# One level of Strassen's algorithm in the second product of four feed-forward layers

## The chip, the cores and the metric

The kernel runs on one core of one Trainium2 chip. What is compared is the time of one execution on the device, in microseconds (us). TensorE (PE) multiplies matrices into PSUM banks, VectorE (DVE) and ScalarE (ACT) work on tiles in SBUF and PSUM, GpSimd (POOL) does a little, and SyncE (SP) issues most of the loads from memory.

## The reference

Two blocks of a network run one after the other on a sequence of 512 tokens of width 1024, in float32. The second block has two layers, and each layer has two feed-forward parts around a mixer. Those four feed-forward parts are the place of the change:

```python
D_FF = 2816
def swiglu_half(x, w1, w3, w2):
    return 0.5 * ((jax.nn.silu(x @ w1) * (x @ w3)) @ w2)

for l in range(2):
    x = layer_norm(ALPHA * x + swiglu_half(x, ffn1_w1[l], ffn1_w3[l], ffn1_w2[l]), ln1_g[l], ln1_b[l])
    ...                                       # mixer, and its own layer norm
    x = layer_norm(ALPHA * x + swiglu_half(x, ffn2_w1[l], ffn2_w3[l], ffn2_w2[l]), ln3_g[l], ln3_b[l])
```

Here x is 512 x 1024, w1 and w3 are 1024 x 2816, and w2 is 2816 x 1024. "The hidden values" are silu(x w1) * (x w3); "the second product" is hidden values times w2.

## The kernel before, in words

Every large product is done in three passes of a rounded type. An operand is split into a high part and a low part (`split`, lines 212 to 215: ACT copies the value to the type `F32R`, DVE subtracts that copy from the value), and `mm3` (lines 240 to 243) adds three matmuls for one: low x high, high x low, high x high. So each 128 x 128 by 128 x 512 step is three matmuls, and each weight tile costs one ACT and one DVE operation before PE can use it.

A feed-forward layer (`ffn`, line 804) goes over the 2816 hidden columns in 11 blocks of 256: block 0 alone, then the pairs (1, 2), (3, 4), (5, 6), (7, 8) and (9, 10). `hidden(c)` makes one block's hidden values: two pieces of w1 and w3 (1024 x 256 each, loaded in halves of 512 KB) against the transposed x, 96 matmuls in four PSUM banks of the pool "mm" (three banks), then on ACT the silu, on DVE the product, and the split into `hh` and `hl`. These lie with the hidden column on the partitions, so that 128 tokens of them are the stationary operand of the second product. For a pair, both hidden blocks come first. Then the second product goes over 4 token tiles x 2 halves of the 1024 output columns; each of the 8 results adds 4 steps of 128 hidden columns (12 matmuls) into a bank of the pool "mx" (five banks), and DVE adds the bank to the residual `xr` (line 848). After the last pair, `lnorm` does the layer norm.

The order in which instructions stand in each engine's queue is set when the kernel is built: a scheduler takes the program, a model of each operation's cost and the free buffers, and puts what it holds to be ready first. Each queue is then worked off strictly in order, and waits on semaphores keep data and buffers safe. Tiles come from pools: a tile of a tag with `bufs=n` waits until one of that tag's n places is released. The pool `WP` has 2 staging tiles (`wst`) and 4 places each for high (`wh`) and low (`wl`) weights; the layer's own weight pool has 3 and 5. All weight loads are issued by SP, in order.

Of the kernel before, what the change touches and what calls it, by code (L numbers as in the profile page):

```python
# [133 lines left out]
def build(ctx, tc, A, out, stage="all"):  # L134
# [24 lines left out]
    def nm(s):  # L159
        uid[0] += 1  # L160
        return f"{s}{uid[0]}"
# [18 lines left out]
    def mmbank():  # L180
        return bank("mm")

    def mxbank():
        return bank("mx")
# [108 lines left out]
    def nat(t):  # L293
        return slice(t * 128, (t + 1) * 128)
# [437 lines left out]
        return nxt  # L732


    def lnorm(t, po, scale, g, b, pl, done):
# [9 lines left out]
        xn = pl.tile([128, D], F32, tag="lnx", name=nm("lnx"), bufs=1)  # L745
        sq = pl.tile([128, D], BF16, tag="lnq", name=nm("lnq"), bufs=1)
# [9 lines left out]
        hc = slice(h * 512, (h + 1) * 512)  # L756
        nc.sync.dma_start(out[0, nat(t), hc], A["xr"][:, t, hc])

    def ln_rows(pl, names, l):
        o = []  # L760
        for n in names:
            r = pl.tile([128, D], F32, name=nm("lnr"))
            nc.scalar.dma_start(r, rows(A[n][l]))
            o.append(r)
        return o
# [6 lines left out]
    def open_ffn(l, f, pre=None):  # L772

        es, w = pre[0:2] if pre else (ExitStack(), None)
        w = w or weights(es, 3, 5, "right")
        return es, w, [Piece(A[f"{f}_{n}_2"][l], 0, 8, 0, 256, wp) for n, wp in (("w1", w), ("w3", WP if pre else w))], []
# [15 lines left out]
    def hidden_half(pl, pre, n0, bufs, sa=None):  # L792

        if not pre[3]:
            pre[3].extend(hidden_tiles(pl, bufs))
# [5 lines left out]
        sa = (pl.tile([128, T], F32, tag="sa", name=nm("sa"), bufs=2) if sa is None else sa).rearrange("p (j n) -> p j n", j=2)  # L801
        act(sa, ab[0], ab[1], hh[:, :, n0:n0 + 256], hl[:, :, n0:n0 + 256])

    def ffn(l, f, ln, pre, ahead=None, scale=None):
# [5 lines left out]
        esf = ExitStack()  # L810
        banks(esf, mm=3, mx=5)
        fp = pool(esf, nm("ffn"), "right", LINE)
        g, b = ln_rows(fp, (ln + "_g_2", ln + "_b_2"), l)

        def hidden(c):

            if c == 0:
                for n0 in (256,) if pre[3] else (0, 256):
                    hidden_half(fp, pre, n0, 3)
                return pre[3]  # L820
            pcs = [Piece(w, 0, 8, c * 256, 256, wf) for w in (w1, w3)]
            hh, hl = hidden_tiles(fp, 3)
            for j in range(2):
                ab = [mmbank() for _ in range(2)]
                for i in range(2):
                    prod(ab[i], pcs[i], j, 0, T)
                act(fp.tile([128, T], F32, tag="sa", name=nm("sa"), bufs=2), ab[0], ab[1], hh[:, j, :], hl[:, j, :])
            return hh, hl

        for cs in ((0,), (1, 2), (3, 4), (5, 6), (7, 8), (9, 10)):  # L830
            hs = [hidden(c) for c in cs]
            p2 = [Piece(w2, 2 * c, 2, 0, 1024, wf if c == 10 else WP) for c in cs]
            if 10 in cs and ahead:
                nxt = ahead(pre)
            nk = 2 * len(cs)
            for t in range(NT):
# [12 lines left out]
                if 10 in cs:  # L849
                    if t > 0 and ahead:  # L850
                        next_tile(t - 1, scale)
                    lnorm(t, lambda h: pos[h], 0.5, g, b, fp, None if ahead else put_out)
        if ahead:
            next_tile(3, scale)
        esf.close()
# [7 lines left out]
    def mixer(l, pre, ahead=None, scale=None):  # L863
# [655 lines left out]
                next_tile(t - 1, scale)  # L1519
            lnorm(t, lambda h: po[h], 1.0, g, b, P4, None if ahead else put_out)  # L1520
        if ahead:
            hidden_half(pool(nxt[0], nm("hid"), "right", LINE), nxt, 0, 1,
                        P4.tile([128, D], F32, tag="lnx", name=nm("sa"), bufs=1)[:, 0:T])
            B["mx"] = B["gd"]
            next_tile(2, scale)
            next_tile(3, scale)
# [51 lines left out]
```

## Time and profile before

| | |
|---|---|
| median of 3 runs | 2773.11 us (2770.71 to 2774.16) |
| the profiled execution | 2771.1 us, span 2769.3 us |
| PE busy | 2722.5 us, 98% of the span, 14736 matmuls |
| DVE busy | 1399.8 us, 51% |
| ACT busy | 999.7 us, 36% |
| POOL busy | 185.8 us, 7% |
| mean DMA rate | 94 GB/s, 16 engines' mean share 31% |

The span runs from the first to the last instruction; the execution's time has a little around it. Busy shares are means over stages with different limits, so a stage is to be read by itself. A PE that is shown busy need not run at its peak, because matmuls overlap: its rate is read from the distance between starts.

### The profile page before, as it was taken

To read this page: it belongs to the slowest core of one execution; us is meant where nothing else is said; L and a number is where in the kernel's file an instruction comes from. 1 tells how busy PE (TensorE), PEld (TensorE's weight loads), DVE (VectorE), ACT (ScalarE), POOL (GpSimd) and SP (SyncE) were. 2 spreads that over 40 slices of the span, in tenths; PEclk is the share of its full clock that TensorE was granted. 3 is DMA by queue.
4 is the path that set the end of the run, shared out by engine and by line. 5 is a ranking of instruction groups with operands and counts; after the bars stand their busy time and mean duration, and the time that the engine had idled before them with its cause. 6 is when DMAs were issued, how large, how long until landed. Compare 5 with 4: busy or idle time off the path is not lost. (4 is left out here: it accounts for less than half of the span.)

```text
span 2769.3 us, 36863 instructions
## 1 busy us (share of the span) xinstructions
PE 2722.5 (98%) x14736; PEld 2224.0 (80%) x14736; DVE 1399.8 (51%) x2698; ACT 999.7 (36%) x1607; POOL 185.8 (7%) x319
## 2 busy tenths in 40 slices
PE   8999999999999999999999999999999999999998
PEld 6779887888888887777888888888887777788887
DVE  6655555344433346865633435334354866643334
ACT  4444553333222234553422224222234553422222
POOL 1000013000000001110100000000000201100000
PEclk9999999999999999999999999999999999999999
DMA  5122222343333223224423333333323323433331
GB/s 165 47 77 70 69 77 88 104 156 101 104 102 91 76 87 91 64 72 138 128 92 95 102 101 99 91 92 97 102 66 89 94 59 129 132 97 92 92 91 46
DMA packets 195003, 260.64 MB, mean 94 GB/s; under 512 B 14376, under 2 KB 153264, under 8 KB 194768
## 3 DMA queue, kind: packets, MB, share of 16 engines
q1 hardware_dynamic: 169200, 221.55, 27.0%
q10 hardware_dynamic: 25632, 36.74, 4.1%
q8 instruction: 116, 1.90, 0.3%
q14 instruction: 55, 0.45, 0.0%
HBM read 246.09 MB, written 11.11 MB: 93 GB/s over the span
## 5 line engine op out<-in xcount | busy, mean ns | idle before, releaser
L215 DVE TENSOR_TENSOR wl<-wst,wh 128x1024 fp32r<-128x1024 f32 (+2 forms) x434 | 516.3, 1192 | 521.4 <-ACT wh L214 520.7
L167 PE MATMUL mm<-xTh,wl 128*128 128x512 f32 (+1 forms) x1984 | 749.6, 378 | 2.2 <-ACT xTh L214 2.1
L167 PE MATMUL mm<-xTl,wh 128*128 128x512 f32 (+1 forms) x1984 | 749.5, 378 | 0.6 <-DVE xTl L215 0.6
L167 PE MATMUL mm<-xTh,wh 128*128 128x512 f32 (+1 forms) x1984 | 746.4, 376 | 0.0
L214 ACT ACTIVATE wh<-wst 128x1024 fp32r<-128x1024 f32 (+2 forms) x434 | 438.9, 1019 | 778.4 <-PE mx L167 327.1
L167 PEld LDWEIGHTS mm<-xTh,wl 128*128 128x128 f32 x1984 | 373.7, 189 | 70.7 <-ACT xTh L214 2.6
L167 PEld LDWEIGHTS mm<-xTl,wh 128*128 128x128 f32 x1984 | 373.8, 188 | 70.3 <-issue 2.9
L167 PEld LDWEIGHTS mm<-xTh,wh 128*128 128x128 f32 x1984 | 373.8, 188 | 66.5
L167 PE MATMUL mx<-wh,hl 128*128 128x512 f32 x704 | 276.6, 393 | 0.0
L167 PE MATMUL mx<-wl,hh 128*128 128x512 f32 x704 | 274.1, 389 | 0.0
L167 PE MATMUL mx<-wh,hh 128*128 128x512 f32 x704 | 271.5, 390 | 0.0
L167 PE MATMUL mm<-wh,xTl 128*128 128x512 f32 (+2 forms) x640 | 254.0, 398 | 0.4 <-DVE xTl L215 0.4
L167 PE MATMUL mm<-wl,xTh 128*128 128x512 f32 (+2 forms) x640 | 248.8, 389 | 0.0
L167 PE MATMUL mm<-wh,xTh 128*128 128x512 f32 (+2 forms) x640 | 245.7, 384 | 0.0
L848 DVE TENSOR_TENSOR xr<-xr,mx 128x512 f32<-128x512 f32 x160 | 109.5, 686 | 206.8 <-PE mx L167 206.8
L789 DVE TENSOR_TENSOR sa<-sa,mm 128x512 f32<-128x512 f32 x88 | 60.5, 687 | 276.7 <-PE mm L167 276.7
L167 PEld LDWEIGHTS mm<-wl,xTh 128*128 128x128 f32 x640 | 144.7, 226 | 18.2 <-issue 5.8
L167 PEld LDWEIGHTS mm<-wh,xTl 128*128 128x128 f32 x640 | 144.2, 226 | 18.7 <-issue 5.2
L167 PEld LDWEIGHTS mx<-wh,hl 128*128 128x128 f32 x704 | 132.1, 188 | 32.3 <-DVE hl L215 5.7
L167 PEld LDWEIGHTS mm<-wh,xTh 128*128 128x128 f32 x640 | 144.7, 226 | 14.5 <-issue 1.8
L167 PEld LDWEIGHTS mx<-wh,hh 128*128 128x128 f32 x704 | 132.1, 188 | 27.8
L167 PEld LDWEIGHTS mx<-wl,hh 128*128 128x128 f32 x704 | 132.2, 188 | 26.5
(396 smaller groups left out, 2731.7 us busy)
## 6 DMA issues: line engine op xcount, KB each, us to landing
wst<-in_ffn_w_dram SPq DMA_DIRECT2D x264, 512.0 KB, 3.7
wst<-in_w_in_dram SPq DMA_DIRECT2D x106, 512.0 KB, 3.7
wst<-in_w_out_dram SPq DMA_DIRECT2D x24, 512.0 KB, 3.4
xd<-xr ACTq DMA_DIRECT2D x8, 512.0 KB, 2.6
wst<-in_w_in_dram SPq DMA_DIRECT2D x16, 256.0 KB, 2.8
lnr<-in_ln_g_dram ACTq DMA_DIRECT2D x6, 512.0 KB, 4.2
lnr<-in_ln_b_dram ACTq DMA_DIRECT2D x6, 512.0 KB, 6.0
ya<-xd ACTq DMA_DIRECT2D x10, 256.0 KB, 2.9
```

Source lines behind the costliest of these rows:

```text
L167: PE.matmul(o, a, b, start=start, stop=stop)
L214: S.activation(hi, src, AF.Copy)
L215: V.tensor_sub(lo, src, hi.bitcast(F32))
L789: V.tensor_mul(sa, sa, pb)
L848: V.tensor_add(xs, xs, po)
```

## The change

In each of the four feed-forward layers the second product of the pairs (1, 2), (3, 4), (5, 6) and (7, 8) is done by one level of Strassen's algorithm, in Winograd's form. The hidden values of a pair are a 2 x 2 array (tokens 0 to 255 and 256 to 511, first and second block); the matching 512 rows of w2 are a 2 x 2 array of quarters (256 rows by 512 columns). Seven products of quarters take the place of eight. Hidden values go in as x1 (tokens 0 to 255 of the first block, "11", and the difference s3), x2 ("12" and "22"), x3 (s2 and s1) and x4 (s4); weights as the quarters 11, 21 and 22 and the sums t1 to t4. Each sum is made in float32 before it is split.

Three of the seven products ("12" by 21, s4 by 22, "22" by t4) belong to one quarter of the output each, and DVE adds them to `xr` straight from PSUM. The other four belong to more than one. They are kept in SBUF tiles (`acc`, 256 tokens x 512 columns each) over all four pairs of the layer, and `joined` adds them to `xr` once, after the last of these pairs. In the first pair ACT copies these four into their tiles; later DVE adds to them.

The layer norm's gain and offset rows are now loaded after that, into the places of `acc`, and its scratch tiles take places of hidden tiles. Blocks 0, 9 and 10 are done as before. The core of the diff (left out: the passing of tags, and of one pool that lets every third set of hidden tiles lie with block 0's):

```diff
+        def raw(c):
+            pcs = [Piece(w, 0, 8, c * 256, 256, wf) for w in (w1, w3)]
+            sa = fp.tile([128, 2, T], F32, tag="sa", name=nm("sa"), bufs=2)
+            for j in range(2):
+                ab = [mmbank() for _ in range(2)]
+                for i in range(2):
+                    prod(ab[i], pcs[i], j, 0, T)
+                S.activation(sa[:, j, :], ab[0], AF.Silu)
+                V.tensor_mul(sa[:, j, :], sa[:, j, :], ab[1])
+                yield sa, j
...
+        def quarters(c):
...
+            for i, j in ((0, 0), (1, 1), (0, 1), (1, 0)):
+                q = (wp if i == j else fp).tile([128, 2, 512], F32, tag="wst", name=nm("wst"), bufs=2)
+                r = (2 * c + 2 * i) * 128
+                nc.sync.dma_start(q, w2[r:r + 256, j * 512:(j + 1) * 512].rearrange("(k p) c -> p k c", p=128))
...
+            parts("11", q11)
+            V.tensor_add(q11, q11, q12)
+            V.tensor_add(q12, q12, q22)
+            parts("t3", q12)
+            parts("21", q21)
+            parts("22", q22)
+            V.tensor_add(q22, q22, q11)
+            V.tensor_add(q21, q21, q22)
+            parts("t1", q11)
+            parts("t2", q22)
+            parts("t4", q21)
...
+        def pair(c):
...
+            V.tensor_sub(s3, sa1[:, :, lo], sa1[:, :, up])
+            split(x1h[:, :, lo], x1l[:, :, lo], sa1[:, :, lo])
+            split(x1h[:, :, up], x1l[:, :, up], s3)
+            w = quarters(c)
+            for sa2, _ in raw(c + 1):
+                pass
+            V.tensor_sub(sa1[:, :, up], sa1[:, :, up], sa2[:, :, up])
+            x2h, x2l = tiles()
+            split(x2h, x2l, sa2)
+            V.tensor_sub(sa1[:, :, lo], sa1[:, :, up], sa1[:, :, lo])
+            V.tensor_add(sa2[:, :, lo], sa2[:, :, lo], sa1[:, :, lo])
...
+            split(x4h, x4l, sa2[:, :, lo])
+            x3h, x3l = tiles()
+            split(x3h, x3l, sa1)
...
+            for x, y, to in (("11", "11", "q1"), ("s3", "t3", "q7"), ("12", "21", (0, 0)), ("s4", "22", (0, 1)),
+                             ("s1", "t1", "q5"), ("s2", "t2", "q6"), ("22", "t4", (2, 0))):
...
+                for t in range(2):
+                    po = mxbank()
+                    for k in range(2):
+                        mm3(po, xh[:, k, nat(t0 + t)], xl[:, k, nat(t0 + t)], wh[:, k, :], wl[:, k, :], k == 0, k == 1)
+                    if type(to) is not str:
+                        o = xr[:, to[0] + t, to[1] * 512:(to[1] + 1) * 512]
+                        V.tensor_add(o, o, po)
+                    elif new:
+                        S.activation(acc[to][:, t, :], po, AF.Copy)
+                    else:
+                        V.tensor_add(acc[to][:, t, :], acc[to][:, t, :], po)
+
+        def joined():
...
+            V.tensor_add(u2, u2, q1)
+            to(0, 0, q1, ALU.add)
+            to(0, 1, q5, ALU.add)
+            to(0, 1, u2, ALU.subtract)
+            V.tensor_add(u2, u2, q7)
+            to(2, 0, u2, ALU.add)
+            to(2, 1, q5, ALU.add)
+            to(2, 1, u2, ALU.subtract)
 
         for cs in ((0,), (1, 2), (3, 4), (5, 6), (7, 8), (9, 10)):
+            if 0 < cs[0] < 9:
+                pair(cs[0])
+                continue
+            if 10 in cs:
+                joined()
             hs = [hidden(c) for c in cs]
```

What this does to the queues, in the pair of blocks 3 and 4 of the first layer. PE before, from the last matmul of the hidden block 4 (`mm_6341`) into the first result of the second product; `hl_6148` and `hh_6147` are the hidden values of block 3, `hl_6284` those of block 4:

```order
L167 MATMUL mm_6341<-xTh,wh_6279 128x512
L167 MATMUL mx_6419<-wh_6397,hl_6148 128x512
L167 MATMUL mx_6419<-wl_6398,hh_6147 128x512
L167 MATMUL mx_6419<-wh_6397,hh_6147 128x512
L167 MATMUL mx_6419<-wh_6403,hl_6148 128x512
L167 MATMUL mx_6419<-wl_6404,hh_6147 128x512
L167 MATMUL mx_6419<-wh_6403,hh_6147 128x512
L167 MATMUL mx_6419<-wh_6409,hl_6284 128x512
```

PE now, from the end of the third product ("12" by 21, bank `mx_6509`, hidden tiles x2) to the start of the fourth (s4 by 22, bank `mx_6517`, hidden tiles `l_6462` and `h_6461`, which are x4); `mm_6608` is the first bank of block 5's hidden product:

```order
L167 MATMUL mx_6509<-wh_6303,hl_6456 128x512
L167 MATMUL mx_6509<-wl_6304,hh_6455 128x512
L167 MATMUL mx_6509<-wh_6303,hh_6455 128x512
L167 MATMUL mm_6608<-xTh,wl_6586 128x512
L167 MATMUL mm_6608<-xTl,wh_6585 128x512
L167 MATMUL mm_6608<-xTh,wh_6585 128x512
L167 MATMUL mm_6608<-xTh,wl_6586 128x512
L167 MATMUL mm_6608<-xTl,wh_6585 128x512
L167 MATMUL mx_6517<-wh_6307,l_6462 128x512
L167 MATMUL mx_6517<-wl_6308,h_6461 128x512
L167 MATMUL mx_6517<-wh_6307,h_6461 128x512
```

Before, a result took 12 matmuls and began with the earlier block's values; now it takes six, and five matmuls of the next block stand in front of the fourth product.

DVE before, around the end of block 4's hidden product (`sa_6390`); `wl_6552` and `wl_6670` are low parts of the weights for the next blocks:

```order
L215 TENSOR_TENSOR wl_6546<-wst_6543,wh_6545 128x1024
L215 TENSOR_TENSOR wl_6552<-wst_6549,wh_6551 128x1024
L789 TENSOR_TENSOR sa_6390<-sa_6390,mm_6341 128x512
L215 TENSOR_TENSOR wl_6670<-wst_6667,wh_6669 128x1024
L215 TENSOR_TENSOR hl_6284<-sa_6390,hh_6283 128x512
L848 TENSOR_TENSOR xr_4184<-xr_4184,mx_6419 128x512
L848 TENSOR_TENSOR xr_4184<-xr_4184,mx_6433 128x512
L848 TENSOR_TENSOR xr_4184<-xr_4184,mx_6447 128x512
```

DVE now, from the end of block 4's hidden product (`sa_6349`; `sa_6174` is block 3's) to x4's low part `l_6462`; `hl_6456` is x2, `hl_6466` x3, `wl_6314` and `wl_6318` the sums t1 and t2, `acc_6032` and `acc_6049` two kept sums:

```order
L830 TENSOR_TENSOR sa_6349<-sa_6349,mm_6403 128x512
L894 TENSOR_TENSOR sa_6174<-sa_6174,sa_6349 128x2x256
L922 TENSOR_TENSOR acc_6032<-acc_6032,mx_6469 128x512
L215 TENSOR_TENSOR hl_6456<-sa_6349,hh_6455 128x1024
L897 TENSOR_TENSOR sa_6174<-sa_6174 128x2x256
L922 TENSOR_TENSOR acc_6032<-acc_6032,mx_6477 128x512
L215 TENSOR_TENSOR wl_6314<-wst_6285,wh_6313 128x1024
L898 TENSOR_TENSOR sa_6349<-sa_6349,sa_6174 128x2x256
L215 TENSOR_TENSOR hl_6466<-sa_6174,hh_6465 128x1024
L215 TENSOR_TENSOR wl_6318<-wst_6287,wh_6317 128x1024
L215 TENSOR_TENSOR l_6462<-sa_6349,h_6461 128x512
L922 TENSOR_TENSOR acc_6049<-acc_6049,mx_6485 128x512
```

Before, one split of hidden values followed the last hidden product; now ten operations follow it up to the low part that the fourth product starts with.

## Rows read from the trace of the kernel before

**Rows 1.** The page's first part: busy us, share of the span, instructions of each engine.

```profile
PE 2722.5 (98%) x14736; PEld 2224.0 (80%) x14736; DVE 1399.8 (51%) x2698; ACT 999.7 (36%) x1607; POOL 185.8 (7%) x319
```

**Rows 2.** Windows: stretch, length, busy PE, PEld, DVE, ACT, POOL (instructions), clock, DMA, GB/s.

```profile
802.73:846.25 43.52, 43.52 (x194) 36.04 (x193) 17.29 (x18) 13.55 (x17) 0.00 (x0) 1.00 0.40 115
846.25:868.14 21.89, 21.89 (x97) 17.94 (x96) 8.07 (x11) 3.42 (x4) 0.00 (x0) 1.00 0.21 62
```

**Rows 3.** Windows over the four pairs of the first and of the last layer.

```profile
671.83:933.56 261.73, 261.73 (x1154) 215.93 (x1152) 99.75 (x111) 67.30 (x80) 0.00 (x0) 1.00 0.32 93
...
2434.26:2695.73 261.47, 261.47 (x1153) 215.75 (x1151) 99.75 (x111) 67.23 (x80) 0.00 (x0) 1.00 0.31 93
```

**Rows 4.** Timeline of PEld and PE (start, us, operation) at a pair's borders.

```profile
802.50 0.19 PEld L167 LDWEIGHTS mm<-xTh,wl 128*128 128x128 f32 x1
...
802.73 0.39 PE L167 MATMUL mm<-xTh,wl 128*128 128x512 f32 x1
...
846.25 0.39 PE L167 MATMUL mx<-wh,hl 128*128 128x512 f32 x1
...
868.14 0.39 PE L167 MATMUL mm<-xTh,wl 128*128 128x512 f32 x1
```

**Rows 5.** Timeline of PE: block 0's second product, first two matmuls and the end.

```profile
660.92 0.40 PE L167 MATMUL mx<-wh,hl 128*128 128x512 f32 x1
661.16 0.40 PE L167 MATMUL mx<-wl,hh 128*128 128x512 f32 x1
...
671.83 0.39 PE L167 MATMUL mm<-xTh,wl 128*128 128x512 f32 x1
```

**Rows 6.** Groups of DVE by form: operation, count, busy us, mean ns, idle before.

```profile
L215 DVE TENSOR_TENSOR wl<-wst,wh 128x1024 fp32r<-128x1024 f32 x394 | 488.2, 1241 | 440.2 <-ACT wh L214 439.7
L848 DVE TENSOR_TENSOR xr<-xr,mx 128x512 f32<-128x512 f32 x160 | 109.5, 686 | 206.8 <-PE mx L167 206.8
...
L1054 DVE TENSOR_TENSOR glog<-glog,msc 128x1024 f32<-128x1024 f32 x2 | 2.4, 1208 | 0.0
```

**Rows 7.** Timeline: operations in a row (x2), and two that depend on each other.

```profile
1740.07 2.36 DVE L215 TENSOR_TENSOR wl<-wst,wh 128x1024 fp32r<-128x1024 f32 x2
...
664.85 1.28 DVE L848 TENSOR_TENSOR xr<-xr,mx 128x512 f32<-128x512 f32 x2
...
931.72 2.01 ACT L214 ACTIVATE wh<-wst 128x1024 fp32r<-128x1024 f32 x2 [18.27 <-PE mx L167]
...
1084.21 0.17 DVE L205 TENSOR_SCALAR spare<-glss 128x16 f32<-128x16 f32 x1
1084.41 0.17 DVE L206 TENSOR_SCALAR glss<-spare 128x16 int32<-128x16 int32 x1
```

**Rows 8.** The page's DMA issues: count, KB each, us to landing.

```profile
wst<-in_ffn_w_dram SPq DMA_DIRECT2D x264, 512.0 KB, 3.7
```

**Rows 9.** Timeline at the start of a pair's second product (blocks 7, 8).

```profile
911.44 0.39 PE L167 MATMUL mm<-xTh,wh 128*128 128x512 f32 x1
911.66 0.39 PE L167 MATMUL mx<-wh,hl 128*128 128x512 f32 x1
...
911.86 0.69 DVE L789 TENSOR_TENSOR sa<-sa,mm 128x512 f32<-128x512 f32 x1 [0.40 <-PE mm L167]
...
911.86 1.06 ACT L214 ACTIVATE wh<-wst 128x1024 fp32r<-128x1024 f32 x1 [1.66 <-PE mm L167]
912.83 0.61 ACT L214 ACTIVATE hh<-sa 128x512 fp32r<-128x512 f32 x1
```

**Rows 10.** Groups of ACT by form: splits of weights and of hidden values.

```profile
L214 ACT ACTIVATE wh<-wst 128x1024 fp32r<-128x1024 f32 x394 | 413.4, 1057 | 734.7 <-PE mx L167 327.1 <-PE mm L167 253.6 <-DMA wst<-in_ffn_w_dram 89.3
L214 ACT ACTIVATE hh<-sa 128x512 fp32r<-128x512 f32 x88 | 54.9, 624 | 222.1 <-DVE sa L789 222.1
```

**Rows 11.** A tile of the first block (ns min/median/max, first and last start); POOL's timeline there.

```profile
L215 DVE TENSOR_TENSOR yla<-y,yha x4: 693/1670/1811, 448.6 to 455.7; 128x512 fp32r<-128x512 f32 x4
...
446.30 5.24 POOL L674 TENSOR_TENSOR y<-y,gatea 128x512 f32<-128x512 f32 x3 [40.25 <-ACT gateb L656]
```

More of the change, by code (lines that the diff above doesn't have):

```diff
@@ L732, in block1, with lnorm @@
         return nxt
-    def lnorm(t, po, scale, g, b, pl, done):
+    def lnorm(t, po, scale, g, b, pl, done, tags=(("lnx", 1), ("lnq", 1))):
         xs = A["xr"][:, t, :]
@@ L775, in open_ffn @@
         w = w or weights(es, 3, 5, "right")
[L776 removed]
+        return es, w, [Piece(A[f"{f}_{n}_2"][l], 0, 8, 0, 256, wp) for n, wp in (("w1", w), ("w3", WP if pre else w))], [], pre[4] if pre else []
     def hidden_tiles(pl, bufs):
@@ L812, in ffn, with tiles @@
         fp = pool(esf, nm("ffn"), "right", LINE)
-        g, b = ln_rows(fp, (ln + "_g_2", ln + "_b_2"), l)
+        turn = [0]
+        def tiles():
+            turn[0] += 1
+            return hidden_tiles(pre[4][0], 1) if pre[4] and turn[0] % 3 == 0 else hidden_tiles(fp, 2 if pre[4] else 3)
+        def raw(c):
[8 more added lines that the diff above has]
+                yield sa, j
         def hidden(c):
@@ L820, in hidden @@
                 return pre[3]
[L821 to L827, printed above, removed]
-            return hh, hl
-        for cs in ((0,), (1, 2), (3, 4), (5, 6), (7, 8), (9, 10)):
+            hh, hl = tiles()
@@ new lines, in hidden, with parts @@
+            for sa, j in raw(c):
+                split(hh[:, j, :], hl[:, j, :], sa[:, j, :])
+            return hh, hl
+        def quarters(c):
+            wp, nst, nw = WP
+            wp = wp.pool
+            st = {}
+            for i, j in ((0, 0), (1, 1), (0, 1), (1, 0)):
+                q = (wp if i == j else fp).tile([128, 2, 512], F32, tag="wst", name=nm("wst"), bufs=2)
+                r = (2 * c + 2 * i) * 128
+                nc.sync.dma_start(q, w2[r:r + 256, j * 512:(j + 1) * 512].rearrange("(k p) c -> p k c", p=128))
+                st[i, j] = q
+            q11, q12, q21, q22 = st[0, 0], st[0, 1], st[1, 0], st[1, 1]
+            of = {}
+            def parts(n, src):
+                of[n] = [wp.tile([128, 2, 512], F32R, tag=tag, name=nm(tag), bufs=nw) for tag in ("wh", "wl")]
+                split(*of[n], src)
+            parts("11", q11)
[9 more added lines that the diff above has]
+            parts("t4", q21)
+            return of
@@ new lines, in ffn @@
+        acc = {}
+        def pair(c):
+            lo, up = slice(0, 256), slice(256, 512)
+            x1h, x1l = tiles()
+            for sa1, _ in raw(c):
+                pass
+            s3 = fp.tile([128, 2, 256], F32, tag="s3", name=nm("s3"), bufs=1)
+            V.tensor_sub(s3, sa1[:, :, lo], sa1[:, :, up])
[3 more added lines that the diff above has]
+            for sa2, _ in raw(c + 1):
+                pass
+            V.tensor_sub(sa1[:, :, up], sa1[:, :, up], sa2[:, :, up])
[3 more added lines that the diff above has]
+            V.tensor_add(sa2[:, :, lo], sa2[:, :, lo], sa1[:, :, lo])
+            x4h, x4l = (fp.tile([128, 2, 256], F32R, tag=n, name=nm(n), bufs=1) for n in ("h4", "l4"))
+            split(x4h, x4l, sa2[:, :, lo])
+            x3h, x3l = tiles()
+            split(x3h, x3l, sa1)
+            xs = {"11": (x1h, x1l, 0), "s3": (x1h, x1l, 2), "12": (x2h, x2l, 0), "22": (x2h, x2l, 2),
+                  "s2": (x3h, x3l, 0), "s1": (x3h, x3l, 2), "s4": (x4h, x4l, 0)}
+            new = not acc
+            for x, y, to in (("11", "11", "q1"), ("s3", "t3", "q7"), ("12", "21", (0, 0)), ("s4", "22", (0, 1)),
+                             ("s1", "t1", "q5"), ("s2", "t2", "q6"), ("22", "t4", (2, 0))):
+                xh, xl, t0 = xs[x]
+                wh, wl = w[y]
+                if new and type(to) is str:
+                    acc[to] = fp.tile([128, 2, 512], F32, tag="acc", name=nm("acc"), bufs=4)
+                for t in range(2):
[9 more added lines that the diff above has]
+                        V.tensor_add(acc[to][:, t, :], acc[to][:, t, :], po)
@@ new lines, in joined, with to @@
+        def joined():
+            q1, q7, q5, u2 = (acc[n] for n in ("q1", "q7", "q5", "q6"))
+            def to(t0, h, a, op):
+                o = xr[:, t0:t0 + 2, h * 512:(h + 1) * 512]
+                V.tensor_tensor(out=o, in0=o, in1=a, op=op)
+            V.tensor_add(u2, u2, q1)
[6 more added lines that the diff above has]
+            to(2, 1, u2, ALU.subtract)
@@ L851, in ffn @@
                         next_tile(t - 1, scale)
-                    lnorm(t, lambda h: pos[h], 0.5, g, b, fp, None if ahead else put_out)
+                    lnorm(t, lambda h: pos[h], 0.5, g, b, fp, None if ahead else put_out, (("sa", 2), ("s3", 1)))
         if ahead:
```

18 lines of the change are left out of this document (11 added, 7 removed).

## The prediction

> **What bounds the kernel now.** I read the page's busy shares first: TensorE (PE) is busy for 98% of the span, DVE for about half [rows 1]. An average can hide a stage with another limit, so I cut one feed-forward layer into its stages by a table of windows. One pair of blocks is 43.52 us of hidden products (192 matmuls) and 21.89 us of second products (96 matmuls; the rows count one or two cut at the edges more). In both PE is busy for the whole stretch, at the full granted clock; DVE works 17.29 and 8.07 us, ACT 13.55 and 3.42 us, POOL nothing [rows 2]. All four pairs together are the same in all four layers, 261.4 to 261.7 us, with PE's busy time equal to the stretch; the first and the last layer stand for the four [rows 3]. So in these 16 pairs, 1046 us of the span, nothing but PE's own rate counts: a matmul that goes is time that goes, as long as the other engines still hand over their operands in time.
>
> The rate is read from starts, since PE's matmuls overlap (each is shown as 0.39 us long). Between the first second-product matmul at 846.25 and the first matmul of the next block at 868.14 lie 96 matmuls, 0.228 us each; between 802.73 and 846.25 lie 192, 0.2267 us each [rows 4]. Each loads its stationary operand 0.23 us ahead of its start [rows 4], so an operand that is late holds up the load first.
>
> **What goes.** A pair now needs seven products of 2 token tiles x 2 k x 3 = 12 matmuls, 84 in place of 96, of the same form (128x128 by 128x512). Twelve fewer in 4 pairs of 4 layers are 192 of PE's instructions. At 0.2272 us (a mean of the two rates) that is 43.6 us, or 2.73 us per pair. Groups of six matmuls that change bank after each, as the new ones do, are in the trace already: block 0's 48 take from 660.92 to 671.83, 0.2273 us each, while DVE works nearly without a pause [rows 5]. So neither the shorter groups nor a busier DVE should cost rate.
>
> The Trainium skill (TensorE: Matmul & The Clock Gate, Back-to-back issue gap) gives about 216 ns for an isolated 512-column matmul and about 131 ns in a sustained stream of load and matmul; the 192 would be worth 41.5 or 25.2 us by that. The trace disagrees with both for this form, so the sum goes by 0.2272.
>
> **What is added, and what covers it.** Per pair, DVE gets 3 more splits and 4 sums of weight quarters (128x1024), hidden splits of two 1024-wide and three 512-wide in place of four 512-wide, 4 sums of hidden values and 6 more evictions (128x512; in a layer's first pair ACT takes the eight of the kept sums, and DVE has six in all instead of eight). A 1024-wide DVE operation takes 1.24 us, a 512-wide one from PSUM 0.69 us [rows 6]; one after the other they start 1.14 and 0.60 us apart [rows 7]. A 1024-wide operation on two plain float operands in SBUF, which the new sums are, stands in the mixer with 1.21 us [rows 6], the same price. So 9 x 1.14 + 9 x 0.60 = 15.7 us more, to 25.4 + 15.7 = 41.1 us in a pair of 65.4 - 2.7 = 62.7 us. ACT gets 3 splits 0.95 us apart [rows 7] and wider hidden splits, to some 21 us. Both have room, so as throughput all this costs nothing. After the last pair eight 1024-wide sums (9.1 us) join the kept products to the residual beside the hidden products of block 9, where DVE works 17.3 of 43.5 us: nothing, again. If that cover were gone they would cost their 9.1 us in each of four layers, 36 us.
>
> The loads are as many and as large as before; a weight load lands in 3.7 us [rows 8]. The quarters' loads go through SP's queue, where each waits for its staging tile. The last of them is let go by the split of the pair before about 11 us after that pair's products begin, some 10 us ahead of its own split and over 50 ahead of its product; behind it stand pieces of hidden weights that PE takes over 30 us later. The rows of the norm's gain and offset are now loaded by ACT's queue only once the joining sums free their tiles, some 24 us after the last pair's products begin, and are wanted over 40 us later. Nothing.
>
> **Where PE can wait.** What is tight is latency. The seven products follow the hidden products directly, and the operands of the third and fourth are only made from the last hidden block. The order lists show PE's queue: products 11, s3 t3, 12 21, then five matmuls of the next block, then the fourth, whose first operand is the low part of x4 (l_6462). DVE's queue shows ten operations between the last hidden product and that. I work it out from T, the start of the first second-product matmul (911.66 in the trace of before). There, DVE's multiplication starts at T + 0.20 and ACT comes to the hidden split at T + 1.17, after a weight split that stays where it is [rows 9]. An operation that waits for another on its own engine starts 0.03 us after its end (0.17 long, 0.20 apart) [rows 7]; so I take it for other engines too (PE's last hidden matmul ends at 911.83, DVE starts at 911.86) [rows 9].
> DVE starts, in us after T: multiplication 0.20; first difference 0.92; eviction 1.55; x2's low part 2.26 (ACT's high part, 1.06 us [rows 10], is ready at 2.23); second difference 3.40; eviction 4.00; t1's low part 4.60; sum 5.74; x3's low part 6.34; t2's low part 7.48; x4's low part 8.62, done at 9.31. ACT is ahead of each: t1's high part from 2.91 (product 1's end), x3's from 4.12, t2's from 5.64 (product 2's end), x4's from 6.61 to 7.24.
> PE: x2 is wanted at 24 x 0.2267 = 5.44 and ready at 3.5. The fourth product would start at 41 x 0.2267 = 9.29 and its weight load at 9.06; the load can go at 9.34. PE waits 0.28 us. In a layer's first pair there are four matmuls in between instead of five, one weight split more and two evictions fewer on DVE: x4 is done at 9.11, the load wanted at 8.84, 0.3 us. Everything on PE stands behind that load. DVE is then four evictions behind, but PE has five banks: the eighth group wants the third's bank at about 10.9, which is emptied at about 9.9; all later ones have more room.
> So 16 x 0.3 = 4.8 us. Neither the DVE sums nor this wait stands in the trace of before. Bounds: no wait (0), up to one whole 1024-wide operation more in DVE's queue than I count, 1.1 us more, 16 x 1.4 = 22 us. Below nothing it can't go, since PE had no wait there that could vanish. I take 4.8, the value nearest to the rows.
>
> Sum, against the profiled execution's 2771.1 us (span 2769.3): 2771.1 - 43.6 + 4.8 = 2732.3. That execution is 2.0 us under the median of the runs, 2773.1; I add this back and predict 2734.
>
> **Rivals.**
> 1. No wait at all: 2771.1 - 43.6 = 2727.5. For it: I am at 0.3 us with ten links, each good to 0.1. Against it: PE's order itself has foreign matmuls put in at this place. 0.13.
> 2. The chain is later by another operation, 1.4 us a pair: 2749. For it: every link waits on another engine, and ACT's weight splits wait for PE to release a product's tiles; one that comes a product later moves everything. Against: the margins of ACT are about 1 us. 0.13.
> 3. PE's rate falls because DVE and ACT now read and write beside it. If the 84 matmuls of a pair took 0.24 us, the step seen in the first microsecond of block 0's products (660.92 to 661.16) [rows 5], that is 1344 x 0.013 = 17 us: 2750. Against: the rest of the same stretch, with DVE just as busy, runs at 0.2267. 0.04.
> 4. Slower: the new DVE operations, eight of the ten in the chain, have two operands in SBUF, and there are rows where such operations take far longer: in the first block four 512-wide ones took 0.69 to 1.81 us, median 1.67, while POOL ran there [rows 11]. At 1.67 / 0.69 = 2.4 times, the eight (7.0 us by starts) take 16.8, PE waits 10 us a pair for the fourth product, and the kernel comes to 2771.1 - 43.6 + 160 = 2888. It decides from 2.73 us of wait a pair; beyond that every pair is slower than before. Against: POOL has no instruction in these stretches [rows 2], and the change adds none. 0.03.
> The Trainium skill (SBUF — State Buffer, SBUF: two separate sides) has this as a rule: a DVE operation with two SBUF inputs and a POOL operation that reads SBUF exclude each other, and the loser waits out the whole instruction. By that too it is POOL that must be there, and it is not.
> 5. It does not do what it says, because something in PE's order takes the 12 matmuls' place. The lists have 192 rows fewer on PE and the same order outside the pairs, so 0.01 for no change, 2771.
>
> **How the numbers follow.** The forecast (waits of 0.1 to 0.9 us a pair, 2729 to 2742) has 0.66; rivals 0.13, 0.13, 0.04, 0.03, 0.01. The range reaches from just under rival 1 to rival 2's and 3's times: 2726 to 2750. A difference of under 0.2%, 5.5 us, can't be told from no change here. Faster by more: all but rivals 4 and 5 and a little of 2 and 3 at their worst, 0.93; within: 0.03; slower: 0.04.
>
> **What would show it.** PE's second-product stretch of a pair should be 84 x 0.227 = 19.1 us, with 0.3 us of wait in front of the fourth product put down to DVE's low part of x4, and the hidden stretch still 43.5. DVE's busy time should rise by about 16 us a pair, ACT's by 5, with no wait of PE on either elsewhere; PE's instructions should be 192 fewer. I am wrong if a wait at the fourth product is over 1 us, if PE waits for evictions or for weights in the hidden stretch, or if starts there are more than 0.230 us apart.

## The result, and the profile after

The changed kernel takes 2740.77 us (median of 4 runs, 2739.23 to 2741.51), the kernel before on the same chip 2771.91 us (4 runs, 2770.16 to 2774.16): a ratio of 0.989, with a 95% interval of 0.9878 to 0.9902. Forecast were 2734 us, with a range of 2726 to 2750. The profiled execution took 2740.6 us, its span 2738.8 us.

The page's first part, and its row for the queue that brings instructions (packets, MB, share of 16 engines), against [rows 1]: PE has 192 instructions fewer, DVE 257 us more work and ACT 88 us more: 16.1 and 5.5 us a pair, with the joining sums shared out over the pairs.

```profile
PE 2688.9 (98%) x14544; PEld 2194.6 (80%) x14544; DVE 1657.0 (60%) x2986; ACT 1088.0 (40%) x1703; POOL 186.4 (7%) x319
...
q8 instruction: 115, 1.88, 0.3%
```

To find where the time went I cut both spans at the same instructions of PE and put the stretches side by side. First the windows of after (columns as in [rows 2]): the four pairs of the first layer, to be held against [rows 3], the same with the rest of that layer, the first mixer, the second mixer, the last layer's pairs.

```profile
673.10:925.39 252.29, 252.29 (x1110) 207.84 (x1109) 153.84 (x174) 89.53 (x104) 0.00 (x0) 1.00 0.30 92
673.10:992.44 319.34, 319.34 (x1417) 263.27 (x1416) 194.97 (x229) 111.17 (x134) 2.23 (x6) 1.00 0.29 91
992.44:1360.17 367.73, 358.55 (x2692) 283.42 (x2691) 243.43 (x529) 171.68 (x289) 53.73 (x78) 1.00 0.33 102
2034.36:2413.94 379.58, 367.23 (x2692) 289.98 (x2691) 244.00 (x529) 171.79 (x289) 52.92 (x78) 0.97 0.32 98
2413.94:2665.97 252.03, 252.03 (x1109) 207.65 (x1108) 153.93 (x174) 89.48 (x104) 0.00 (x0) 1.00 0.31 92
```

Then the windows of before for the first layer's pairs with the rest of the layer, and for both mixers:

```profile
671.83:1001.73 329.90, 329.90 (x1466) 272.31 (x1464) 132.92 (x159) 89.20 (x110) 2.23 (x6) 1.00 0.29 86
1001.73:1373.99 372.26, 361.28 (x2692) 285.47 (x2691) 240.69 (x527) 171.54 (x289) 53.75 (x78) 0.99 0.33 102
2069.14:2434.26 365.12, 357.11 (x2693) 281.70 (x2692) 241.34 (x527) 171.71 (x289) 53.61 (x78) 1.00 0.34 103
```

A feed-forward layer became 10.56 us shorter (329.90 to 319.34), the four together 42.1 us. But the second mixer, in which PE has the same order of work (DVE's and ACT's differ only in its first 25 and last 35 us), became 14.5 us longer (365.12 to 379.58) at a granted clock of 0.97, and the first 4.5 us shorter. The start of the program and its end add 1.3 and 0.4 us. -42.1 + 14.5 - 4.5 + 1.7 = -30.4, the difference of the spans (30.5). So the question is not Strassen's: why does the same mixer take 365 us once and 380 us another time?

The windows of after around the second mixer's two solve stages, with the stage of before that answers to the first of them as the last row:

```profile
2208.00:2213.00 5.00, 2.66 (x102) 2.04 (x102) 0.69 (x3) 2.67 (x7) 0.00 (x0) 1.00 0.33 101
2213.00:2223.00 10.00, 10.00 (x120) 7.83 (x120) 2.01 (x5) 5.08 (x13) 0.00 (x0) 0.54 0.11 29
...
2308.00:2322.00 14.00, 11.68 (x126) 9.42 (x127) 2.91 (x5) 7.00 (x15) 0.00 (x0) 0.55 0.19 67
```

```profile
2243.00:2255.00 12.00, 11.93 (x251) 9.88 (x250) 3.85 (x9) 10.07 (x27) 1.82 (x1) 1.00 0.19 58
```

In each stage PE first stands still, then runs for some 10 to 14 us at the lower of its two levels (0.50, 1.2 GHz), while before stays at 1.00. Over the whole second mixer PE is 23.9 us at the lower level, before not at all. The solve stages are hundreds of 32x32 matmuls with groups of large ones between. PE's timeline shows the pause itself; in brackets is the idle time and what ended it. After, in the two stages:

```profile
2209.56 0.70 PE L167 MATMUL gd<-yw,fw 32*32 32x32 f32 x49
2212.60 0.26 PE L167 MATMUL gd<-yw,fw 32*32 32x32 f32 x6 [2.34 <-issue]
...
2307.10 0.72 PE L167 MATMUL gd<-yw,fw 32*32 32x32 f32 x52
2310.32 0.32 PE L167 MATMUL gd<-yw,fw 32*32 32x32 f32 x3 [2.50 <-issue]
```

Before, in the first stage; the second has none:

```profile
2240.78 0.50 PE L167 MATMUL gd<-yw,fw 32*32 32x32 f32 x36 [0.55 <-issue]
```

So 4.3 of the 14.5 us are time in which PE stands still (2.34 and 2.50 against 0.55); the other 10.2 us go with the lower clock. The first mixer's gain is of the same kind. There the kernel before has two pauses and 10.2 us at the lower level, the changed kernel one pause (last row) and 3.4 us:

```profile
1174.92 0.25 PE L167 MATMUL gd<-yw,fw 32*32 32x32 f32 x4 [2.08 <-issue]
1274.81 0.53 PE L167 MATMUL gd<-yt,ke 32*32 32x32 f32 x13 [2.00 <-issue]
...
1262.77 0.25 PE L167 MATMUL gd<-yf,fv 32*32 32x32 f32 x4 [1.87 <-issue]
```

"Issue" means that no engine and no transfer of data ended the wait; the pause even lies in the middle of a run of equal matmuls. I counted PE's own instructions in the trace (a weight load, a matmul and a semaphore instruction are one each). The changed kernel pauses at its 13761st instruction, in the first mixer, and at the 23489th and 25281st; the kernel before at its 11713th, 13761st and 23489th. All of them are 193 more than a multiple of 256. And the queue q8 moves 1.88 MB in 115 packets, 16 KB each: 29,466 instructions of PE divided by 256 are 115.1. PE's instructions come in pages of 256, and it stood at the end of a page. In all thirteen traces of this study there are 35 such pauses of 0.5 us or more in the solve stages, and every one is at that place. The Trainium skill (Runtime: NRT & Kernel Launch, Instruction fetch mechanics) gives the same blocks of 16 KiB or 256 instructions, and says that crossing from one to the next is mostly hidden. The first agrees with the trace, the second fails in these stages.

That makes a testable theory. The change takes matmuls out of PE's stream ahead of the mixers (276 instructions up to the second one, semaphores included), so page ends fall on other instructions of an unchanged stage. Theory A: the page's place in the stage decides. Theory B: the moment in time, or chance. Theory C: the change's tiles or loads disturb the mixer.

### The profile page after: what moved, and what is told of

The parts are those of the page before. It is cut to its first block, busy times and chain, and to the rows that moved or that the text cites. A ratio compares the mean times of both kernels' runs of the same rounds, so it can differ in the third digit from the quotient of the medians.

```text
span 2738.8 us, 36804 instructions
## 1 busy us (share of the span) xinstructions
PE 2688.9 (98%) x14544; PEld 2194.6 (80%) x14544; DVE 1657.0 (60%) x2986; ACT 1088.0 (40%) x1703; POOL 186.4 (7%) x319
## 3 DMA queue, kind: packets, MB, share of 16 engines
q8 instruction: 115, 1.88, 0.3%
## 5 line engine op out<-in xcount | busy, mean ns | idle before, releaser
L215 DVE TENSOR_TENSOR wl<-wst,wh 128x1024 fp32r<-128x1024 f32 (+2 forms) x482 | 569.2, 1188 | 465.1 <-ACT wh L214 454.1
L214 ACT ACTIVATE wh<-wst 128x1024 fp32r<-128x1024 f32 (+2 forms) x482 | 489.7, 1023 | 752.1 <-PE mm L167 450.1
L167 PEld LDWEIGHTS mm<-xTh,wl 128*128 128x128 f32 x1984 | 373.6, 188 | 70.9 <-ACT xTh L214 2.6
L167 PE MATMUL mx<-wh,hl 128*128 128x512 f32 x576 | 225.1, 391 | 0.0
L167 PE MATMUL mx<-wl,hh 128*128 128x512 f32 x576 | 224.2, 389 | 0.0
L167 PE MATMUL mx<-wh,hh 128*128 128x512 f32 x576 | 224.1, 389 | 0.0
L830 DVE TENSOR_TENSOR sa<-sa,mm 128x512 f32<-128x512 f32 x80 | 55.0, 687 | 233.9 <-PE mm L167 233.9
L829 ACT ACTIVATE sa<-mm 128x512 f32<-128x512 f32 x80 | 47.8, 597 | 200.4 <-PE mm L167 200.4
L167 PEld LDWEIGHTS mx<-wh,hl 128*128 128x128 f32 x576 | 108.1, 188 | 23.6 <-DVE hl L215 1.5
L167 PEld LDWEIGHTS mx<-wh,hh 128*128 128x128 f32 x576 | 108.1, 188 | 22.6
L167 PEld LDWEIGHTS mx<-wl,hh 128*128 128x128 f32 x576 | 108.2, 188 | 22.0
```

Of the source, the lines that this page charges most:

```text
L167: PE.matmul(o, a, b, start=start, stop=stop)
L214: S.activation(hi, src, AF.Copy)
L215: V.tensor_sub(lo, src, hi.bitcast(F32))
L829: S.activation(sa[:, j, :], ab[0], AF.Silu)
L830: V.tensor_mul(sa[:, j, :], sa[:, j, :], ab[1])
```

## Experiments

The expectations count instructions in the built program, where some matmuls stand once that the trace shows several times; differences between kernels are the same in both.

**Ten useless matmuls.** They go between the two mixers, into the second product of blocks 9 and 10 of the third layer:

```diff
                     po = mxbank()
-                    for k in range(nk):
+                    for k in [None] * (10 if (l, f, cs[0], t, h) == (1, "ffn1", 9, 0, 0) else 0) + list(range(nk)):
+                        if k is None:
+                            mm(po, hs[0][1][:, 0, nat(0)], p2[0].at(0)[0][:, 0:512])
+                            continue
```

> The changed kernel with ten matmuls more (128x128 by 128x512) in PE's queue, in the third feed-forward layer, between the two mixers; their results are overwritten. Everything else stands in the same order on every engine. In the traces of before and after PE stands still without a releaser only in the mixers' solve stages, and each time at the same place modulo 256 of its own instructions (a weight load and a matmul count one each), with a 16 KB transfer of the instruction queue just under way. Theory A (the place of the 256-instruction pages decides): twenty instructions more put the second mixer on the same place as in the kernel before (20868 against 21124, 256 apart), where it took 365.1 us instead of 379.6; ten matmuls cost 2.3 us; so 2740.8 - 14.5 + 2.3 = 2728.6, and the pauses of 2.3 and 2.5 us in the second mixer with the half clock behind them are gone. Theory B (the pauses come with the moment in time, or by chance) and theory C (the change's own tiles or loads disturb the mixer): 2740.8 + 2.3 = 2743.1, second mixer near 379.

Measured: 2726.07 us, ratio 0.984 (0.9826 to 0.9855). More work made the kernel 14.7 us faster than the changed one (the kernel before, run beside each, differs by 0.7 us). Its second mixer:

```profile
2031.14:2397.14 366.00, 357.31 (x2692) 281.83 (x2691) 243.82 (x529) 171.68 (x289) 53.61 (x78) 1.00 0.32 102
```

**128 of them**, a whole page, 29 us later: the same edit with 128 for 10.

> The same with 128 matmuls more in place of ten: 256 instructions, so the second mixer comes 29.1 us later, but on the same place of the pages as in the changed kernel. Theory A: both pauses of the second mixer stay at the same instructions, the stage takes 379 to 380 us again, and the time is 2740.8 + 29.1 = 2769.9. Theory B (the moment decides): the pauses move, vanish or multiply; the second mixer takes anything from 365 to 385 us, 2755 to 2775. Theory C: 2769.9 as well.

Measured: 2763.32 us (2758.24 to 2769.96), the profiled execution 2770.0 with the second mixer below. The pauses (2.04 and 3.04 us) stand in the same two runs of matmuls as in the changed kernel, 256 instructions on. That execution is where theory A put it; the other five are 3 to 12 us shorter, with a mean granted clock of 0.994 to 0.999 against its 0.993, and of these there is no trace. Their spread is also what theory B allowed. So the run shows the place of the pauses in one execution, and that the price of a bad place is not the same in each.

```profile
2061.91:2443.30 381.39, 368.76 (x2692) 291.31 (x2691) 244.03 (x529) 171.93 (x289) 52.94 (x78) 0.96 0.31 98
```

**The kernel before, put on the bad place**: the same edit with 118, in the kernel before.

> The kernel before, without any of the change, with 118 matmuls more at the same place: 236 instructions, which puts its second mixer on the place of the pages that the changed kernel has (21360 against 20848, 512 apart). 118 x 0.2272 = 26.8 us of work. Theory A: the kernel before now falls into the same two pauses of 2.3 to 2.5 us and loses 14.5 us in the second mixer: 2771.9 + 26.8 + 14.5 = 2813. Theories B and C: 2771.9 + 26.8 = 2798.7, second mixer near 365.

Measured: 2808.26 us, ratio 1.0134 (1.0119 to 1.0149). Without a line of the change the second mixer takes 380.15 us, with pauses of 2.04 and 3.60 us, so theory C falls. B falls as far as the moment goes: two kernels below, on places 177 and 178 (x3 first, sums not kept), begin the second mixer at 2034.30 and 2034.25 us and have no pause of 0.5 us in it, while the changed kernel, on place 158, begins it at 2034.36 and has two (a place is counted from the last page end; the table below has them all). Theory A holds for where PE stands still; chance is left in what a pause costs. In the profiled execution (2809.8) most of the rest of the way to 2813 is the first mixer, 369.45 us here and 372.26 before.

```profile
2092.76:2472.91 380.15, 366.88 (x2693) 289.83 (x2691) 241.46 (x527) 172.00 (x289) 52.31 (x78) 0.97 0.32 99
```

**Strassen in the last layer alone**, which no mixer follows:

```diff
-            if 0 < cs[0] < 9:
+            if 0 < cs[0] < 9 and (l, f) == (1, "ffn2"):
                 pair(cs[0])
                 continue
-            if 10 in cs:
+            if 10 in cs and acc:
                 joined()
```

> Strassen's form in the last feed-forward layer alone, which no mixer follows; the other three layers take their pairs as before, with the hidden values' tiles and the norm's rows handled as in the changed kernel. If the gain of the change is made in the pairs and lost in the second mixer: 10.5 us of a layer, 2771.9 - 10.5 = 2761.4 (2760.5 to 2762.5). If instead each layer is worth a quarter of the measured 31.1 us: 2764.1. By my forecast's terms (12 x 4 x 0.2272 less four waits of 0.3 us): 9.7 us, 2762.2.

Measured: 2762.36 us, ratio 0.9969 (0.9958 to 0.9981), which alone can't tell 10.5 from 7.8 us. The trace can: from the last layer's first pair to the end of PE's work before took 326.79 us, this kernel 316.27, 10.5 less.

**A longer chain to x4.** Sixteen useless matmuls stand in the third layer as above (not shown).

```diff
             V.tensor_add(sa2[:, :, lo], sa2[:, :, lo], sa1[:, :, lo])
+            V.tensor_sub(sa2[:, :, lo], sa2[:, :, lo], sa1[:, :, lo])
+            V.tensor_add(sa2[:, :, lo], sa2[:, :, lo], sa1[:, :, lo])
```

> The changed kernel with two more 512-wide operations in DVE's chain to x4 (the second difference is taken off and added again), about 1.2 us by starts. The scheduler answers by putting 17 to 19 more matmuls of the next block in front of the fourth product, 4 us. Sixteen matmuls in the third layer keep the second mixer on the place of the pages that it has in the kernel before (against the kernel with ten: 1.4 us of work more). Theory: the wait at the fourth product was a matter of the place in PE's queue; it goes, and each of the four layers' pairs take 0.1 to 0.8 us less than the 252.2 us of the changed kernel (16 waits of 0.1 to 0.2 us in all); time 2726 + 1.4 - 1 to 3 = 2725 to 2727. Rival: the chain is still late, 1.1 us a pair more: pairs of 256 us a layer, 2744.

One execution, 2727.5 us; the first layer's row is below, 318.65 against 319.34 in the changed kernel. The waits did not go wholly: the loads wait 0.75 us in the four pairs in place of 1.39, which is about the 0.7 us that the layer gained.

```profile
672.04:990.69 318.65, 318.65 (x1418) 263.35 (x1416) 200.19 (x237) 111.63 (x134) 2.23 (x6) 1.00 0.28 91
```

**The sums not kept.** The diff is against the changed kernel; ten useless matmuls stand in the third layer as above (not shown):

```diff
                 pair(cs[0])
+                joined()
+                acc.clear()
                 continue
-            if 10 in cs:
-                joined()
```

> The changed kernel (with the ten matmuls more, so that the second mixer stands as in the kernel before) with one part undone: the four kept sums are not kept through the layer, but joined to the residual after each pair, and ACT copies all of them anew. That gives DVE the eight 1024-wide sums (9.1 us) four times a layer in place of once, less eight evictions that go to ACT in the later pairs. Theory: DVE has room beside the next block's hidden products, so it costs nothing: 2726 (2724 to 2729), pairs 252 us a layer. Rival: the sums stand in DVE's queue ahead of the multiplications that empty the banks of the hidden products, and PE waits for part of it; all of it would be 3 x 4 x 9.1 = 109 us, a fifth of it 22 us, 2748.

Measured: 2726.85 us, ratio 0.985 (0.9834 to 0.9867), the same as with the sums kept (2726.07). DVE works 17 us more in the pairs (153.84 to 171.24) and PE does not notice:

```profile
672.43:924.76 252.33, 252.33 (x1111) 207.84 (x1109) 171.24 (x178) 102.33 (x129) 0.00 (x0) 1.00 0.31 98
```

**x3's product ahead of x4's.** Ten useless matmuls as above (not shown).

```diff
-            for x, y, to in (..., ("s4", "22", (0, 1)), ("s1", "t1", "q5"), ...):
+            for x, y, to in (..., ("s1", "t1", "q5"), ("s4", "22", (0, 1)), ...):
```

> The changed kernel (with the ten matmuls more) with the products in another order: s1 by t1 (x3, ready one operation earlier on DVE) fourth, s4 by 22 (x4) fifth. Theory: x3's low part is ready about 1.1 us before x4's and x4 has twelve matmuls more of time, so the loads wait for neither: no row of a weight load waiting for x4, pairs 0.1 to 0.8 us a layer shorter than 252.2, time 2723 to 2726. Rival: the third place moves up too far, as the scheduler takes the five foreign matmuls away, and the load waits for x3 instead, 0.3 us or more: 252.2 or up, 2726 to 2735.

One execution, 2725.9 us, the layer below: 0.4 us less. No load waits for x3 or x4; three wait up to 0.3 us for DVE's evictions instead.

```profile
672.78:991.71 318.93, 318.93 (x1418) 263.46 (x1416) 195.03 (x229) 111.13 (x134) 2.23 (x6) 1.00 0.28 91
```

**Loads of an eighth in the second mixer.** The kernel leaves out seven eighths of the columns of these weights.

```diff
-                nc.sync.dma_start(st, src[...])
+                m = ncol // 8 if slim[0] else ncol
+                nc.sync.dma_start(st[:, :, 0:m], src[...])
...
+                    split(hi.rearrange(v, r=8), lo.rearrange(v, r=8),
+                          st[:, :, 0:m].unsqueeze(2).to_broadcast([128, self.hk, 8, m]))
```

> The changed kernel without the ten matmuls, so on the place of the pages where it had both pauses. Its weight loads in the second mixer's solve stages and after (the four inner projections and the output product) bring an eighth of the columns, 64 KB in place of 512 KB, repeated eight times by the split; the order on PE is the same up to the stages. This tells what makes the transfer of instructions late. Theory A1 (the page is simply used up too fast: 256 instructions, most of them tiny, in less time than a transfer takes): pauses of 2.0 to 2.5 us at the same two instructions (places 23489 and 25281 of PE's stream), second mixer 375 to 381. Theory A2 (the transfer also stands behind the weight loads that fill the DMA engines just then): pauses shrink to under 1 us, the clock stays up, second mixer 365 to 368, time 2741 - 13 = 2728. Chance of A2 one half.

One execution, 2734.7 us, second mixer 373.6. The pauses stay at the same two instructions, shorter by 0.6 us each (2.34 to 1.76, 2.50 to 1.95). After the first the clock stayed up, after the second it fell. So the weight loads do not make the pauses, and A2, which put them under 1 us, falls. Whether they lengthen them is not shown: six kernels (the changed one, those with 10, 128, 64 and 32 more, and this one) have the same instructions on PE up to the pause in the first mixer, and there it took 0.82 to 1.87 us, with the first mixer 364.9 to 368.4 us long.

```profile
2212.25 0.26 PE L167 MATMUL gd<-yw,fw 32*32 32x32 f32 x6 [1.76 <-issue]
...
2305.44 0.25 PE L167 MATMUL gd<-yw,fw 32*32 32x32 f32 x3 [1.95 <-issue]
```

**Put together, and two places more.** x3 first with ten narrow matmuls; then 64 and 32 narrow ones in the changed kernel.

```diff
-                            mm(po, hs[0][1][:, 0, nat(0)], p2[0].at(0)[0][:, 0:512])
+                            mm(po[:, 0:64], hs[0][1][:, 0, nat(0)], p2[0].at(0)[0][:, 0:64])
```

> The changed kernel with what the runs so far point to: the product of x3 ahead of that of x4, and ten matmuls more in the third layer, now 64 columns wide. In the trace with ten wide ones, matmuls of 256 columns start 0.11 us apart, so ten of 64 columns are taken at no more than 1.1 us in place of 2.3. Theory: pairs 251.8 us a layer (0.4 less than in the changed kernel, four times), second mixer 365 to 366: against the run with ten wide ones (2726) 1.6 + 1.2 us less, 2723 (2721 to 2726), faster than both kernels. Rival: the narrow ones shorten PE's cover at the place where they stand, and the pauses come back with the chance of the runs: 2730 to 2737.

Measured: 2725.57 us (5 runs, 2722.15 to 2728.33), ratio 0.984 (0.9826 to 0.9853). It beats both kernels, but not measurably the one with ten wide matmuls: the pairs gave their 0.4 us a layer (318.90), the first mixer had a pause of 1.80 us in the profiled run and took 368.6 us.

> The changed kernel with 64 narrow matmuls more (129 instructions with one semaphore), 64 x 0.06 to 0.11 = 4 to 7 us of work. The second mixer's solve stages then begin 31 and 39 places behind a page's start, next to where the first mixer's begin in the changed kernel (20 and 28), which there had no pause or 0.6 us in the first stage and 0.9 to 1.9 in the second. Theory A: the same here, second mixer 365 to 368, and none of the two pauses of the places 158 and 166. Rival (the place says nothing across mixers): pauses of any size.

> The same with 32 narrow ones (65 instructions with one semaphore), 2 to 3.5 us of work. The stages begin 223 and 231 places behind a page's start, where no run so far has been: 45 places on from the kernel before (178 and 186: 0.6 us and none) and 53 short of the first mixer's. Theory A tells no size beforehand, only that any pause stands at the end of a page (places 193 modulo 256) with a transfer of instructions under way. If the places between two good ones are good, 365 to 367.

One execution each, 2737.3 and 2730.5 us; second mixers 370.2 and 366.3. At 31 and 39 the second pause is 2.25 us and the mixer 2 us over the forecast, which had no such pause there: the place is not a full rule for the size. The narrow matmuls themselves cost more than the 4 to 7 and 2 to 3.5 us forecast: from the end of the first mixer to the start of the second it is 10.1 and 5.0 us longer than in the changed kernel, and PE's clock fell to 0.50 there, for 6.8 and 3.4 us.

All traces together, worked out from each one's transfers on q8. The place is that of a stage's first tiny matmul behind the last page end. "Lead" is how long before the pause's beginning the transfer on q8 began that was last to start; "until" is from that start to PE's next matmul.

```
kernel            places    pauses          lead             until           clock  second mixer
before            178, 186  0.55            2.28             2.82            1.00   365.1
changed           158, 166  2.34,2.50       0.21,-0.17       2.55,2.33       0.97   379.6
ten               178, 186  0.66            2.13             2.79            1.00   366.0
128               158, 166  2.04,3.04       0.37,-0.77       2.41,2.27       0.96   381.4
before and 118    158, 166  2.04,3.60       0.32,-1.18       2.36,2.42       0.97   380.2
last layer alone  177, 185  0.63            2.24             2.87            1.00   365.9
longer chain      178, 186  0.87            2.19             3.06            1.00   368.3
sums not kept     178, 186  none                                             1.00   366.2
x3 first          177, 185  none                                             1.00   365.0
thin loads        158, 166  1.76,0.52,1.95  0.63,1.81,0.47   2.39,2.33,2.42  0.99   373.6
put together      178, 186  0.70            2.12             2.82            1.00   367.2
64 narrow         31, 39    0.73,2.25       1.60,0.00        2.33,2.26       0.99   370.2
32 narrow         223, 231  0.65,1.24       1.76,1.32        2.41,2.57       1.00   366.3
```

PE goes on 2.3 to 3.1 us after the transfer's start. The pause is what is left of that when the page is used up: 0.5 to 0.9 us with a lead of about 2, over 2 us with none. What the places do can be read from the same traces. In front of all ten pauses of the table that are over 1.2 us PE ran two pages in a row in 3.1 to 4.4 us each, and the last transfer began 5.5 to 7.3 us after the one before it. In front of six of the eight shorter ones the page before the last took 16 to 21 us; in front of the other two the transfers began 4.2 and 4.9 us apart. So what sets the places apart is, for the most part, whether one page or two in a row are full of tiny matmuls. Why the second of two such transfers begins so late is open.

## Why the prediction came out as it did

It held, by its range, and its forecast was 6.8 us too low. In the profiled executions, 2732.3 against 2740.6, the 8.3 us are two errors of opposite sign: the pairs gained 3.3 us more than forecast, and 11.6 us were lost outside them. That the time lies in the range, and even in the 2729 to 2742 us that had most of the chance, is luck: no term stood for the loss.

**The bound** was right: the pairs are 252.3 us long with PE busy in all of it, and 1109 matmuls in 252.29 us are 0.2275 us each. Neither shorter groups nor a busier DVE cost rate: products 1 to 3 of the second pair take from 779.44 to 787.60, 36 matmuls at 0.2267. So rival 3 falls.

**The chain to x4** came out link by link. DVE after in the second pair, where T is 779.44:

```profile
779.64 0.69 DVE L830 TENSOR_TENSOR sa<-sa,mm 128x512 f32<-128x512 f32 x1 [0.35 <-PE mm L167]
780.36 0.69 DVE L894 TENSOR_TENSOR sa<-sa,sa 128x512 f32<-128x512 f32 x1
781.00 0.69 DVE L922 TENSOR_TENSOR acc<-acc,mx 128x512 f32<-128x512 f32 x1
781.73 1.23 DVE L215 TENSOR_TENSOR hl<-sa,hh 128x1024 fp32r<-128x1024 f32 x1
782.87 0.68 DVE L897 TENSOR_TENSOR sa<-sa 128x512 f32<-128x512 f32 x1
783.47 0.68 DVE L922 TENSOR_TENSOR acc<-acc,mx 128x512 f32<-128x512 f32 x1
784.07 1.22 DVE L215 TENSOR_TENSOR wl<-wst,wh 128x1024 fp32r<-128x1024 f32 x1
785.21 0.69 DVE L898 TENSOR_TENSOR sa<-sa,sa 128x512 f32<-128x512 f32 x1
785.81 1.22 DVE L215 TENSOR_TENSOR hl<-sa,hh 128x1024 fp32r<-128x1024 f32 x1
786.95 1.22 DVE L215 TENSOR_TENSOR wl<-wst,wh 128x1024 fp32r<-128x1024 f32 x1
788.08 0.68 DVE L215 TENSOR_TENSOR l<-sa,h 128x512 fp32r<-128x512 f32 x1
```

Forecast for the last start was T + 8.62; it is T + 8.64. All between are within 0.03 us, and rivals 2 and 4 fall with them: operations on two SBUF operands take 0.69 and 1.22 us here.

**The wait at the fourth product** is there, on the weight load. It stands idle for 0.35 us, 0.04 of which lies between any two loads, so it is 0.31 us late where 0.28 was forecast. PEld after, from the last of the five foreign loads on:

```profile
788.28 0.19 PEld L167 LDWEIGHTS mm<-xTl,wh 128*128 128x128 f32 x1
788.82 0.19 PEld L167 LDWEIGHTS mx<-wh,l 128*128 128x128 f32 x1 [0.35 <-DVE l L215]
```

The term of 4.8 us was mis-sized all the same. The step that failed is the sentence that below nothing it can't go, "since PE had no wait there that could vanish". Before, each pair had such a wait, 3.2 us behind the first second-product matmul, where the later block's low part comes in; in the second pair:

```profile
783.98 0.19 PEld L167 LDWEIGHTS mx<-wh,hl 128*128 128x128 f32 x1 [0.27 <-DVE hl L215]
```

I had read windows and a mean of 0.228 us a matmul there, and not asked PEld's own timeline why it was above 0.2267. At 0.2267 the 1152 matmuls of the four pairs would take 261.16 us and took 261.73, 0.14 us a pair over; the 1109 after would take 251.41 and took 252.29, 0.22 over. What the change adds is 0.08 us a pair, 1.3 us in all. 16 pairs x (12 x 0.2267 - 0.08) = 42.2 us, which the four layers show.

**What covers the DVE work** held with room to spare: the run that joins the sums after each pair costs nothing either. So the price I gave for lost cover was never near, and keeping the sums through the layer saves no time that these runs show.

**The sum** failed at a step that it does not even name. It takes the 1723 us outside the pairs as unchanged, and rival 5 leans on "the same order outside the pairs". PE's order is the same, and the time is not: 14.5 us in the second mixer, -4.5 in the first. Shown by the runs: twenty instructions more bring the second mixer back to 366 us, 236 more put the mixer of the kernel before to 380, and with 256 more it takes 381 in the profiled execution, though other executions of that kernel are up to 12 us shorter. None of the rivals had it; the range held it because rivals 2 and 3, which did not happen, were priced at 2749 and 2750.

## What to carry to other kernels

A change that takes instructions out of an engine's queue moves everything behind it on the pages in which they are fetched; where a later stage is dense in tiny instructions, cut the trace of both kernels at the same instructions and look there for "issue" pauses before explaining the change by itself. A few instructions of padding, tried at two or three counts, can be worth more than the last edit: ten useless matmuls gave 14.7 us, for this program and until an edit ahead moves the pages again. And where a stretch runs some thousandths of a microsecond above the rate of its neighbours, ask the load's timeline for the wait in it before calling it free of waits.

## What the runs showed of the hardware

PE's instructions come in transfers of 16 KB, 256 of them, and at the 35 pauses it goes on 2.2 to 3.1 us after such a transfer starts. In the feed-forward layers, where a page is 128 matmuls of 0.227 us, nobody sees that; among hundreds of 32x32 ones it is a pause of up to 3.6 us. The clock adds to the price: in the second mixer it fell to 0.50 behind every pause of 1.95 us or more and behind none of 1.76 or less; in the first it fell behind some of 0.8 to 1.0 us, and stayed up behind one of 2.63 in the kernel before with 118 matmuls more. What one pause costs is therefore uneven: two of 2.3 and 2.5 us made 14.5 us, one of 2.25 us in the run with 64 narrow matmuls 4 to 5 us.
